# Moving three of the seven down-projection steps, and one hidden-layer copy, inside a feed-forward's step order

## The chip, the cores and the metric

The kernel runs on one core of a Trainium2 chip. The metric is the device time of one execution in microseconds (us), the median of several runs. Five engines work beside each other, each taking its own instructions strictly in the order in which they stand in the program for that engine: TensorE (PE, matrix products, with PEld for the loading of weights), VectorE (DVE), ScalarE (ACT), GpSimd (POOL) and SyncE (SP, which here issues DMA transfers). Products land in PSUM, which has eight banks of 128x512 fp32; everything else lives in SBUF.

## The reference

The reference is a two-layer decoder trunk on a sequence of 1024 tokens of width 1024, in fp32. Layer 0 mixes tokens with a sparse attention of three branches, layer 1 with dilated windows over shared keys and values. After each attention comes the same feed-forward, and that is where the change is:

```python
def swiglu(h, w_up, w_down):
    a, b = jnp.split(h @ w_up, 2, axis=-1)
    return (jax.nn.silu(a) * b) @ w_down
...
x = x + swiglu(rmsnorm(x, norm_ffn[layer]), ffn_w_up[layer], ffn_w_down[layer])
```

The hidden width is 2816, that is 22 inner blocks of 128 hidden columns.

## The kernel before, in words

Every fp32 operand of a product is split in two fp32r parts, a high one (`ph`, written by ACT, line 1002) and a low rest (`pl`, a subtraction on DVE, line 1003); `Pairs` at line 996 does that. One logical product of 128x128 by 128x512 is then three matmuls (`mm3`, lines 375 to 377: high x high, high x low, low x high).

The feed-forward (`ffn`, line 1369) takes the inner blocks two at a time. Both the up- and the down-projection are done as 2x2 block products in Strassen's form as Winograd wrote it, so seven products stand in place of eight.

**The hidden steps.** For each inner block j, `cols_steps` (line 1195) makes seven steps, in the order m1 m2 m5 m6 m7 m4 m3. Each is 12 matmuls: four products that add into one PSUM bank. m1, m6, m7 and m4 add into one bank, `ux` in the steady part; m2 has a bank `uy` for itself; m5 and m3 add into another tile of the same bank `uy`. The results are drained between: after m1, ACT copies the bank to `d0` (line 1218); after m2, DVE adds m2's bank to `d0` (line 1227) and ACT applies the SiLU (line 1415); after m6 and m7, ACT copies the bank again to `d1` and `c` (lines 1257, 1266), and DVE adds m5's bank to `c` (line 1267); after m4 and m3, DVE finishes (lines 1283 and 1417). The step m6 is fed by a GpSimd subtraction (line 1250), which overwrites the block that m5's operands are made from.

**The down steps.** The finished pair of blocks is four 128x512 tiles `u`, and four tiles `wd` hold its rows of the down-projection. `rows_steps` (line 1029) makes seven steps, called D0 to D6 here in the order in which `down_steps` (line 1431) leaves them. Each is 12 matmuls: four rows t, three matmuls each. D0, D3, D4 and D6 add into the four banks dx0 to dx3; D1, D2 and D5 use the two banks dr0 and dr1 in turn. After each row, DVE adds the bank to the residual stream `xr` (line 1061): four additions a step, and eight in D2. D2 and D3 are fed by four GpSimd operations each (lines 1069 to 1079). D0's preparation also issues the four weight transfers of its pair (`load_down`, line 1389), and, in layer 0, two transfers that another stage needs.

**The order.** The down steps of one pair are dealt out among the 14 hidden steps of the next pair. The loop at line 1460 builds one list `seq`, and `staged` (line 1019) runs it: the preparation of step k+1 (pairs, GpSimd operations, transfers) is written ahead of the products of step k. This is the written order. The build schedules it with a timeline simulation (`schedule_with_timeline_sim=True` in `kernel`): an instruction that the simulated timeline sees ready can go ahead of one written earlier, down to single matmuls, so that the order on an engine in the trace is near the written order and not equal to it. After the build each engine's order is fixed.

**The memory blocks.** `u` and the other temporaries are `scratch` blocks. `ut` deals out six of them (`scratch[7:13]`), four to a pair, so that the third and fourth tile of a pair, `u[2]` and `u[3]`, are the first and second tile of the pair before it, which the down steps are reading meanwhile. The second block of a pair has `base = 2` and keeps its `d0` in `u[2]`, its `d1` in `u[3]`. D3's preparation is the last reader of the old tile behind `u[2]`. `misc["c"]` is `scratch[13]`, the one block that holds `c` from m7 to m3.

In what follows the steps of the second block of a pair have a prime: m1', m2' and so on.

Of the kernel before, what the change touches and what calls it, by code (L numbers as in the profile page):

```python
# [299 lines left out]
def trunk(ctx, tc, I, out):  # L300
# [1068 lines left out]
    def ffn(p, scratch, B, xr, layer):  # L1369
# [4 lines left out]
        misc = dict(c=scratch[13], s1=scratch[14], s2=None)  # L1374
# [4 lines left out]
        def load_up(j, q, t=None):  # L1379

            t = wu() if t is None else t
            r, c = q % 2 * 512, q // 2 * FH + j * 128
            v = t.rearrange("p (a n) -> p a n", n=128)
            nc.sync.dma_start(v, up[r:r + 512, c:c + 128].rearrange("(a p) n -> p a n", p=128))
            k = q % 2 * 4
            nc.gpsimd.tensor_mul(v, v, gains[:, k:k + 4].unsqueeze(2).to_broadcast([128, 4, 128]))  # L1386
            raw.setdefault(j, []).append(t)
# [9 lines left out]
        def hidden(j, u):  # L1397

            def ahead(f):
                if j == 1:  # L1400
                    raw[2].clear()
                if 0 < j < NJ - 1:
                    for q in range(3):
                        load_up(j + 1, q)
                return f()

            def tmp(n):
                if n in ("d0", "d1"):
                    return u[base + int(n[1])]
                return scratch[15] if (j, n) == (0, "c") else misc[n]  # L1410

            def done(a, r, C):
                t = u[base + r]
                if a == 0:
                    nc.scalar.activation(t, C, AF.Silu)
                else:
                    nc.vector.tensor_mul(t, t, C)

            base = 2 * (j % 2)
            banks = {0: ("dx2", "uy", "uy"), 1: ("dx3", "ux", "uy")}.get(j, ("ux", "uy", "uy"))  # L1420
            steps = cols_steps(banks, "m1 m2 m5 m6 m7 m4 m3", pairs, tmp, B.ops, lambda: raw[j], done)
            i = 2 if j in (1, 2) else 0
            steps[i] = steps[i][0], lambda f=steps[i][1]: ahead(f)

            def m4(f=steps[5][1]):
                if j == 0:
                    raw[1].clear()
                if j + 1 < NJ:
                    for q in range(3 if j else 0, 4):
                        load_up(j + 1, q)  # L1430
                return f()
            steps[5] = "m4", m4
            return steps

        def down_steps(j, u):
            st = {}

            def first():
                w, last = load_down(j)
                if layer == 0 and 2 <= j < 18:  # L1440
                    for a in ((s1, LA, L1, W1 + 2), (s2, LA + L1, L2, W2 + 1)):
                        bias_skewed(*a, j - 2, last)
                st["s"] = rows_steps(("dr0", "dr1"), pairs, lambda s, i: own("t" + s), [(tuple(u), tuple(w))], xr)
                st["s"].insert(4, st["s"].pop(5))
                return st["s"][0]()

            return [first] + [lambda i=i: st["s"][i]() for i in range(1, 7)]
# [7 lines left out]
        seq, prev, pairs_of = [], [], {}  # L1455
# [4 lines left out]
        for j in range(0, NJ, 2):  # L1460
            if j >= 4:
                u = [ut() for _ in range(4)]
                pairs_of[j] = u, [hidden(j, u), hidden(j + 1, u)]
            u, us = pairs_of[j]
            if j == 0:
                norm = B.half(xr, 1, ("dr0", "dr1", "dx0", "dx1"),
                              ([own("ta")[:], own("tb")[:]] + wd.parts[:2],
                               wd.parts[2:3] + [scratch[10]] + scratch[12:14]),
                              sums=scratch[4:7] + scratch[15:])
                early = [us[1], pairs_of[2][1][0]]  # L1470
                us[0] = [("", f) for f in B.first_steps(us[0], norm, [f for c in early for _, f in c[:2]])]
                for c in early:
                    del c[:2]
            steps = [f for _, f in us[0] + us[1]]
            if j == 2:
                steps.insert(0, prev.pop(0))
            for i, f in enumerate(steps, j == 2):
                seq.append(f)
                if i % 2 and prev:
                    seq.append(prev.pop(0))  # L1480
            seq += prev
            prev = down_steps(j, u)
# [31 lines left out]
    def dense(layer, w, x_src, oT, tail, near, far):  # L1514

        lo, hi = slice(0, 512), slice(512, 1024)
        scratch = [oT[:, 4 * b + i, h] for h in (lo, hi) for b in range(2) for i in range(4)]
        with ExitStack() as c:
            c.push(open_banks(*[(n,) for n in ("dx0", "dx1", "dx2", "dr0", "dr1", "ux", "dx3", "uy")]))
            B = Blocks()  # L1520
            B.add(pool(c, "fb", far), ("B11", "B21"))
            xr = pool(c, "fx", far).tile([128, NT, D], F32, name="xr")
            out_proj(c, near, far, B, xr, oT, w, x_src, layer and 7)
            with ExitStack() as cu:
                p = pool(cu, "fu", near)
                with ExitStack() as ch:
                    B.add(pool(ch, "fb2", far), second)
                    last = ffn(p, scratch, B, xr, layer)
                with ExitStack() as ch:
                    pz = pool(ch, "fz", far)  # L1530
                    begin, finish = tail
                    last(pz, *begin(pz, B, xr))
            finish(c, B, xr, scratch)
# [436 lines left out]
```

## Time and profile before

| what | value |
|---|---|
| median of 3 runs | 2914.61 us (2912.68 to 2917.57) |
| profiled execution, its own time | 2911.7 us |
| its span, first to last instruction | 2909.9 us |
| granted TensorE clock, mean | 0.99 |
| PE busy, share of the span | 2817.3 us, 97% |
| DVE busy | 2255.6 us, 78% |
| ACT busy | 1520.9 us, 52% |
| POOL busy | 1540.8 us, 53% |
| feed-forward of layer 0, steady part | about 905 to 1428 us of the span |
| feed-forward of layer 1, steady part | about 2346 to 2868 us |

How to read it: matmuls are pipelined and their ends are modelled, so that a busy PE is not one at its peak. The number that tells is how fast matmuls follow each other: where nothing holds them up, 12 of them start within 2.72 us in these stages. In a timeline, a row is one instruction or a run of the same kind: start, duration, engine, line, operation, what it writes and reads, count, and in brackets the idle time before it and what ended it. In a table by windows, each row is a stretch of time with the busy time of each engine in it and the number of instructions.

### The profile page before, as it was taken

The page shows a single profiled execution, that of the slowest core. Times are in us where ns is not written, and L with a number is a line of the kernel's source. Part 1 is how long each engine was busy: PE and PEld are TensorE (multiplying, and loading weights), DVE is VectorE, ACT ScalarE, POOL GpSimd, SP SyncE. Part 2 cuts the span into 40 slices and gives each one's busy share as a digit, 9 for nine tenths or more (in the row PEclk, how much of TensorE's full clock was granted, in tenths as well). Part 3 has the DMA queues.
Part 4 walks back from the last instruction along what each step waited for, and adds up shares of the span by engine and source line. Part 5 has one row for each costly group of instructions (what it writes and reads, how often), then busy time and mean ns, then how long its engine had stood idle before and what let it go on. Part 6 is the DMA issues. An engine that isn't in the chain of part 4 may idle for free.

```text
span 2909.9 us, 43844 instructions
## 1 busy us (share of the span) xinstructions
PE 2817.3 (97%) x14766; PEld 2376.1 (82%) x14766; DVE 2255.6 (78%) x4465; ACT 1520.9 (52%) x3314; POOL 1540.8 (53%) x1776
## 2 busy tenths in 40 slices
PE   7999999999999999999999999899999999999997
PEld 6988899998877888888787888788877788888885
DVE  5441999997488888988876777598965888888887
ACT  5431888886443333333554444689855433333334
POOL 2134877873165555555546786455522655555551
PEclk8999999999999999999999999999999999999999
DMA  5756243212122322231225555966521221111112
GB/s 161 237 156 190 67 111 89 59 26 117 30 69 66 83 62 66 62 83 52 95 80 146 161 167 160 281 194 184 142 88 37 73 61 51 55 55 58 51 44 76
DMA packets 266833, 294.46 MB, mean 101 GB/s; under 512 B 18099, under 2 KB 209475, under 8 KB 266608
## 3 DMA queue, kind: packets, MB, share of 16 engines
q1 hardware_dynamic: 246960, 231.50, 27.5%
q0 software_dynamic: 19648, 60.16, 6.9%
q8 instruction: 117, 1.92, 0.3%
q14 instruction: 108, 0.88, 0.1%
HBM read 228.49 MB, written 78.81 MB: 106 GB/s over the span
## 4 chain that ended last, share of the span: by engine, by line
PE 72%; DVE 16%; ACT 4%; issue 3%; DMA 2%; POOL 2%; SPq 1%; DVEq 0%; ACTq 0%; POOLq 0%
PE ux L375 5%; PE ux L376 5%; PE ux L377 5%; DVE pl L1003 5%; PE pt L485 5%; DVE xr L1061 4%; PE uy L375 4%; PE uy L376 4%; PE uy L377 4%; PE dx L376 4%; PE dx L377 4%; PE dx L375 3%; PE dr L375 3%; PE mm L375 3%; PE mm L376 3%
## 5 line engine op out<-in xcount | busy, mean ns | idle before, releaser
L1003 DVE TENSOR_TENSOR pl<-oT,ph 128x512 fp32r<-128x512 f32 x325 | 323.6, 1016 | 73.2 <-ACT ph L1002 64.1
L1002 ACT ACTIVATE ph<-oT 128x512 fp32r<-128x512 f32 x325 | 196.4, 626 | 221.8 <-PE ux L376 60.2
L485 PE MATMUL pt<-ident,P 128*128 128x128 f32 x1536 | 260.3, 277 | 4.8 <-DVE tl L349 2.3
L1003 DVE TENSOR_TENSOR pl<-oTb,ph 128x512 fp32r<-128x512 f32 x235 | 218.2, 954 | 50.6 <-ACT ph L1002 42.3
L1002 ACT ACTIVATE ph<-oTb 128x512 fp32r<-128x512 f32 x235 | 140.4, 625 | 177.3 <-PE ux L376 52.5
L1061 DVE TENSOR_TENSOR xr<-xr,dr 128x512 f32<-128x512 f32 x320 | 204.6, 679 | 29.2 <-PE dr L377 29.2
L1386 POOL TENSOR_TENSOR oT<-oT,gffn 128x512 f32<-128x512 f32 x92 | 106.7, 1168 | 205.5 <-DMA oT<-in_ffn_w_up_dram 168.5
L349 DVE TENSOR_TENSOR tl<-pt,th 128x512 fp32r<-128x512 f32 (+1 forms) x320 | 194.2, 625 | 20.9 <-ACT th L348 17.3
L485 PEld LDWEIGHTS pt<-ident,P 128*128 128x128 f32 x1536 | 181.5, 141 | 28.3 <-POOL P L924 4.1
L924 POOL TENSOR_SCALAR P<-P,sm,gates 128x384 f32<-128x384 f32 (+7 forms) x256 | 182.6, 723 | 38.6 <-DVE sm L922 32.6
L1061 DVE TENSOR_TENSOR xr<-xr,dx 128x512 f32<-128x512 f32 x320 | 200.1, 680 | 2.4 <-PE dx L377 1.8
L348 ACT ACTIVATE th<-pt 128x512 fp32r<-128x512 f32 (+1 forms) x320 | 168.4, 545 | 42.9 <-PE pt L485 33.0
L1386 POOL TENSOR_TENSOR oTb<-oTb,gffn 128x512 f32<-128x512 f32 x92 | 103.8, 1138 | 154.5 <-DMA oTb<-in_ffn_w_up_dram 134.7
L920 ACT ACTIVATE P<-P,m 128x384 f32<-128x384 f32 (+7 forms) x256 | 171.1, 671 | 12.4 <-DVE m L918 9.0
L1761 ACT ACTIVATE P<-P,st 128x384 f32<-128x384 f32 (+2 forms) x256 | 139.4, 548 | 6.2 <-DVE st L1756 5.2
L376 PE MATMUL dx<-pl,ph 128*128 128x512 f32 x352 | 139.3, 396 | 1.0
L377 PE MATMUL dx<-ph,pl 128*128 128x512 f32 x352 | 136.5, 391 | 0.0
L510 PE MATMUL o<-tl,V 128*128 128x256 f32 x476 | 136.3, 304 | 0.0
L509 PE MATMUL o<-th,V 128*128 128x256 f32 x476 | 135.9, 300 | 0.2 <-DVE oTb L522 0.2
L1756 DVE CUSTOM_DVE_ANT_0 P<-s,T 128x384 f32<-128x384 f32 (+2 forms) x256 | 115.7, 478 | 15.9 <-PE s L1812 5.2
L1002 ACT ACTIVATE ph<-wd 128x512 fp32r<-128x512 f32 x86 | 53.7, 629 | 115.5 <-PE ux L376 55.0
L914 DVE CUSTOM_DVE_ANT_0 P<-s,T 128x256 f32<-128x256 f32 (+3 forms) x192 | 101.8, 551 | 6.4 <-PE s L912 4.6
(951 smaller groups left out, 9530.9 us busy)
## 6 DMA issues: line engine op xcount, KB each, us to landing
qB<-xr POOLq DMA_DIRECT2D x96, 256.0 KB, 5.1
oT<-in_ffn_w_up_dram SPq DMA_DIRECT2D x92, 256.0 KB, 3.1
oTb<-in_ffn_w_up_dram SPq DMA_DIRECT2D x92, 256.0 KB, 3.0
Q<-qB SPq DMA_DIRECT2D x40, 512.0 KB, 7.8
wd<-in_ffn_w_down_dram SPq DMA_DIRECT2D x66, 256.0 KB, 2.5
oT<-in_b_w_q_dram SPq DMA_DIRECT2D x48, 256.0 KB, 4.0
K<-kBs SPq DMA_DIRECT2D x40, 256.0 KB, 9.6
wraw<-in_a_w_in_dram SPq DMA_DIRECT2D x18, 512.0 KB, 4.7
```

What stands on the lines that cost most here:

```text
L348: nc.scalar.activation(H_, src, AF.Copy)
L349: nc.vector.tensor_sub(L_, src, f32(H_))
L375: nc.tensor.matmul(ps, lh, rh, start=first, stop=False, skip_group_check=bool(shared))
L376: nc.tensor.matmul(ps, lh, rl, start=False, stop=False, skip_group_check=bool(shared))
L377: return nc.tensor.matmul(ps, ll, rh, start=False, stop=last, skip_group_check=bool(shared))
L485: nc.tensor.transpose(ps[:, i * 128:(i + 1) * 128], b, ident)
L920: nc.scalar.activation(P[:, e, :n], P[:, e, :n], AF.Exp, bias=mm[:, e:e + 1], scale=-1.0, accum_out=sm[:, e:e + 1])
L924: nc.gpsimd.tensor_scalar(P[:, e, :n], P[:, e, :n], sm[:, e:e + 1], gt(g, t, br, 2 * hp + e, 1), op0=OP.mult, op1=OP.mult)
L1002: nc.scalar.activation(like(h), src, AF.Copy)
L1003: (eng or nc.vector).tensor_sub(like(l), src, f32(like(h)))
L1061: nc.vector.tensor_add(xs, xs, banks[t])
L1386: nc.gpsimd.tensor_mul(v, v, gains[:, k:k + 4].unsqueeze(2).to_broadcast([128, 4, 128]))
```

## The change

Two edits, both in `ffn`.

```diff
             def tmp(n):
+                if n == "d0" and j > 4 and j % 2:
+                    return misc["c"]
                 if n in ("d0", "d1"):
                     return u[base + int(n[1])]
                 return scratch[15] if (j, n) == (0, "c") else misc[n]
...
             for i, f in enumerate(steps, j == 2):
                 seq.append(f)
-                if i % 2 and prev:
+                if i in (2, 3, 5, 8, 10, 11, 13) and prev:
                     seq.append(prev.pop(0))
```

The written order for every pair from j = 4 on (nine pairs in each layer):

```
before: m1 m2 D0 m5 m6 D1 m7 m4 D2 m3 m1' D3 m2' m5' D4 m6' m7' D5 m4' m3' D6
after:  m1 m2 m5 D0 m6 D1 m7 m4 D2 m3 m1' m2' D3 m5' m6' D4 m7' D5 m4' m3' D6
```

D0, D3 and D4 each stand one hidden step later. For the pair j = 2, which has lost its first two hidden steps to an earlier place, the order starts with D0 in both versions, and there D1, D4 and D5 stand one step later. Nothing is added or taken away: the same matmuls, splits, additions and transfers are issued.

The other edit concerns the second block of each pair from j = 5 on. Its `d0`, the copy that ACT makes of m1', is kept in `misc["c"]` and no longer in `u[2]`; the SiLU then reads it there and writes `u[2]` as before. With D3 written behind m2', m1's copy into `u[2]` would be written ahead of D3's preparation, which still reads the old tile there.

## The prediction

> **What bounds the kernel now.** I read the page first, then the feed-forward in windows, then single engines in timelines. The page says that PE is the engine to watch:
>
> ```profile
> span 2909.9 us, 43844 instructions
> ...
> PE 2817.3 (97%) x14766; PEld 2376.1 (82%) x14766; DVE 2255.6 (78%) x4465; ACT 1520.9 (52%) x3314; POOL 1540.8 (53%) x1776
> ```
>
> A busy PE is no measure here, so I cut the steady feed-forward at the first matmul of m1 and of m1'. A first half (m1 to m1') holds 114 matmuls, which the weight loads count, and a second half 138. The windows of the first halves, one row and the sum of all 18 (16 with 114 loads, the pair j = 4 of each layer with 110):
>
> ```profile
> 1021.11:1046.98 25.87, 25.87 (x115) 21.42 (x114) 21.64 (x28) 9.24 (x16) 17.64 (x14) 1.00 0.17 52
> ...
> sum 463.72, PE 463.72 PEld 383.97 DVE 382.72 ACT 165.37 POOL 315.68; mean PE 25.76 PEld 21.33 DVE 21.26 ACT 9.19 POOL 17.54
> ```
>
> 25.87 us for 114 matmuls is 0.227 us each, 2.72 us for a step of 12: PE never waits there. The second halves that end in another pair's m1, one row and the sum of all 16:
>
> ```profile
> 1046.98:1079.84 32.86, 32.57 (x139) 25.68 (x138) 30.88 (x45) 12.81 (x22) 15.24 (x11) 1.00 0.32 80
> ...
> sum 518.20, PE 515.15 PEld 411.07 DVE 475.79 ACT 205.19 POOL 233.95; mean PE 32.20 PEld 25.69 DVE 29.74 ACT 12.82 POOL 14.62
> ```
>
> At 0.2267 us, 138 matmuls take 31.28 us, and 16 halves 500.5 us; they took 518.2. So PE loses 17.7 us there, 1.1 us a pair, and that is what a reordering can win. The timeline of PE shows one of the places, where D4 (`dx`) and m6' (`ux<-T2`) are cut into each other:
>
> ```profile
> 1056.54 1.01 PE L375 MATMUL dx<-ph 128*128 128x512 f32 x2
> 1057.66 0.50 PE L375 MATMUL ux<-T2h,ph 128*128 128x512 f32 x1
> 1057.99 0.39 PE L376 MATMUL ux<-T2l,ph 128*128 128x512 f32 x1
> 1058.22 0.62 PE L375 MATMUL dx<-ph 128*128 128x512 f32 x2
> 1058.92 0.50 PE L376 MATMUL dx<-pl,ph 128*128 128x512 f32 x1
> ```
>
> What they wait for is in DVE's timeline, which has no idle time in brackets: two `pl`, D3's four additions, and only then D4's `pl<-wd`, after which (1058.79) PE goes on; m2's addition, which frees `uy` for m5', is later still.
>
> ```profile
> 1054.50 1.29 DVE L1003 TENSOR_TENSOR pl<-oT,ph 128x512 fp32r<-128x512 f32 x2
> 1055.71 2.48 DVE L1061 TENSOR_TENSOR xr<-xr,dx 128x512 f32<-128x512 f32 x4
> 1058.10 0.77 DVE L1003 TENSOR_TENSOR pl<-wd,ph 128x512 fp32r<-128x512 f32 x1
> 1058.79 0.68 DVE L1003 TENSOR_TENSOR pl<-oT,ph 128x512 fp32r<-128x512 f32 x1
> 1059.39 0.67 DVE L1227 TENSOR_TENSOR oT<-oT,uy 128x512 f32<-128x512 f32 x1
> ```
>
> The windows from the end of m2' to the start of m5' (24 matmuls: D4 and m6'), one row and the sum of 16:
>
> ```profile
> 1056.50:1063.15 6.65, 6.43 (x26) 4.53 (x25) 6.65 (x12) 2.94 (x5) 4.83 (x5) 1.00 0.40 118
> ...
> sum 98.78, PE 96.93 PEld 69.98 DVE 98.78 ACT 45.60 POOL 70.50; mean PE 6.06 PEld 4.37 DVE 6.17 ACT 2.85 POOL 4.41
> ```
>
> 384 matmuls would take 87.0 us; they took 98.8, so 11.7 of the 17.7 us go here, 0.73 us a pair and 1.2 at most, and DVE is busy for all of the 98.78 us. The kernel is bound by PE, except where DVE is late, and that is at D4. Most of the rest is at m4', which waits for ACT's copy of the bank that m7' filled: a row of PE, and the windows from the last matmul of m7' to the second of m4' (5 matmuls), summed over the same 16 pairs.
>
> ```profile
> 1070.18 0.50 PE L375 MATMUL ux<-T4h,ph 128*128 128x512 f32 x1
> ```
>
> ```profile
> sum 23.67, PE 22.47 PEld 13.79 DVE 13.19 ACT 17.46 POOL 18.28; mean PE 1.40 PEld 0.86 DVE 0.82 ACT 1.09 POOL 1.14
> ```
>
> 80 matmuls would take 18.1 us, so 5.5 us are lost there.
>
> **The change part by part.** No instruction is added, so the sum is made of waits that go, stay or come.
>
> *D3 and D4 one step later.* What DVE has to do, counted from the code, as additions and `pl` of a step: D2 10; D0, D1, D3 to D6 6 each; m3 3; m2, m7, m4 2; m1, m5, m6 1: 70 over the 21 steps of a pair, 3.33 a step. How far the demand stands above its mean after each step, beginning at m1: before, it reaches +1.0 after D2, +1.0 after D3 and 0 after D4; after the change +1.0 after D2, -0.3 after D3 and -2.3 after D4, since m2' and m6', which ask little of DVE, now stand ahead of them. An operation costs DVE 0.60 us undisturbed (four additions from 1055.71 to 1058.10) and 0.75 in the mean: 21.64 + 30.88 us of the two rows above over 70. So DVE is ahead by 1.3 operations, 1.0 us, at D3 and 2.3 operations, 1.75 us, at D4. That is more than the mean and the worst stall at D4 (0.73 and 1.2 us). Also, m5' now has D3's 2.72 us between it and m2', in which its bank is freed; before, it had nothing. I take the whole stall: -11.7 us. Bounds: 0, if DVE's lateness moves with it, and -11.7.
>
> *m6' right behind m5' in the written order.* The GpSimd subtraction for m6' waits for m5's `pl`:
>
> ```profile
> 1055.27 1.67 POOL L1250 TENSOR_TENSOR oT<-oT 128x512 f32<-128x512 f32 x1 [7.16 <-DVE pl L1003]
> ```
>
> With 0.63 us on ACT and 0.68 on DVE this chain is 3.0 us, 0.3 more than one step. Started at 1055.27 as now, it is done at 1058.3. In the new order the same three steps m1', m2' and D3 are over at 1056.5, m5' takes until 1059.3, and m6' is due then, so I take 0. If m5's `pl` comes only just in time for m5', it costs 0.3 us a pair, 5.4 us for 18.
>
> *D0 behind m5.* D0 no longer stands between m2 and m5, which use the same bank `uy`. In DVE's timeline of a first half there is spare time just then:
>
> ```profile
> 1027.73 1.23 DVE L1003 TENSOR_TENSOR pl<-oT,ph 128x512 fp32r<-128x512 f32 x1 [2.06 <-ACT ph L1002]
> 1028.89 0.68 DVE L1227 TENSOR_TENSOR oT<-oT,uy 128x512 f32<-128x512 f32 x1
> ```
>
> The schedule can pull D0's matmuls ahead of m5, as it already let m6 pass m5. The one spot where the trace has m5 too near to m2 is the start of layer 0's feed-forward:
>
> ```profile
> 814.59 0.47 PE L375 MATMUL dx<-T2h,ph 128*128 128x512 f32 x1
> 815.92 0.50 PE L375 MATMUL uy<-T1h,ph 128*128 128x512 f32 x1 [0.85 <-DVE oT L1227]
> ```
>
> The step from one to the next is 1.33 us in place of 0.23: 1.1 us lost, and up to 1.2 with the slow second matmul behind a stall. Bounds 0 and +1.2 a pair; nearest is the first half as it is, with no loss, so I take 0.1, +1.8 us for 18 pairs.
>
> *m4'.* m7' D5 m4' is written as before: 0. Bound -5.5, if six of D5's matmuls come to stand between, 1.36 us, against four now.
>
> *The pair j = 2.* D5 waits 1.53 us for DVE (886.35 against 884.43: 1.7 us lost), and D2 0.83 us for its bank:
>
> ```profile
> 866.60 0.50 PE L375 MATMUL dr<-ph 128*128 128x512 f32 x1 [0.83 <-DVE xr L1061]
> ```
>
> ```profile
> 884.43 0.39 PE L376 MATMUL ux<-T2l,ph 128*128 128x512 f32 x1
> 886.35 0.50 PE L376 MATMUL dr<-pl,ph 128*128 128x512 f32 x1 [1.53 <-DVE pl L1003]
> ```
>
> D5 stands a step later, so half of 2 x 1.7 us goes (-1.7; bounds 0 and -3.4). D1 moves one step towards D2, with the same two banks: +0.8 (bounds 0 and +1.7).
>
> *`d0` in `misc["c"]`.* ACT's copy of m1' now waits until DVE has read `c`:
>
> ```profile
> 1050.90 0.69 DVE L1417 TENSOR_TENSOR oT<-oT 128x512 f32<-128x512 f32 x1
> ```
>
> ```profile
> 1051.30 0.58 ACT L1218 ACTIVATE oT<-ux 128x512 f32<-128x512 f32 x1
> ```
>
> The read ends at 1051.59, 0.3 us after the copy began. Queued behind it on ACT are two `ph`, whose `pl` DVE reached only at 1054.50; that hides it. 0; without that cover, 0.3 x 18 = +5.4 us.
>
> *Transfers and queues.* D0's four transfers, six in layer 0, pass m5, which issues none on SP. D0 has no GpSimd work; D3's four operations pass m2', which has none. D4 has none either. What D4 frees is the block of its second weight tile, refilled at once:
>
> ```profile
> 1058.89 0.34 SPq L1394 DMA_DIRECT2D wd<-in_ffn_w_down_dram  x1
> ```
>
> ```profile
> 1062.90 1.30 POOL L1070 TENSOR_TENSOR tb<-wd,wd 128x512 f32<-128x512 f32 x1
> ```
>
> A step later it is issued at 1061.6; the GpSimd operation that reads it would start 1 to 2 us later. Its result is wanted by the next pair's D2, some 30 us on: 0.
>
> *Sum:* -11.7 + 1.8 - 1.7 + 0.8 = -10.8 us. The profiled execution took 2911.7 us, 1.8 more than its span, so it becomes 2900.9. The median of the runs is 2.9 us above that execution, so the median becomes 2903.8, and I say 2904. A change under 0.2%, 5.8 us, can't be told from none.
>
> **The rivals.**
>
> *All of it goes.* D4 now stands ahead of m7', so that D5's matmuls may all fall between m7' and m4', and the order m7', six of `dr`, m4' runs without loss in the first halves. For it: those halves lose nothing. Against it: D5 is written where it was. -11.7 - 5.5 - 3.4 = -20.6: 2894.
>
> *The lateness moves along.* DVE is busy for 475.79 of 518.20 us in the second halves, 92%. If its backlog there is made by the long `pl` and not by the order, the same 0.7 us is lost at m5' or m6':
>
> ```profile
> L1003 DVE TENSOR_TENSOR pl<-oT,ph 128x512 fp32r<-128x512 f32 x20 | 20.9, 1070 | 2.1 <-ACT ph L1002 2.1
> L1061 DVE TENSOR_TENSOR xr<-xr,dx 128x512 f32<-128x512 f32 x17 | 10.6, 679 | 0.0
> ```
>
> In one pair the `pl` take 1070 ns in the mean, the additions 679. Against it: the lead of 1.75 us at D4. 2914 to 2916.
>
> *It does nothing.* The schedule sets the machine's order from what is ready, and may give nearly the old one: 2914.6. Against it: between steps that are all ready, the written order decides.
>
> *Slower: m5 waits for m2's bank.* If the schedule keeps m5 in front of D0, or DVE's addition comes later on the chip than the schedule thought, PE stands at m5 in the first halves, 1.2 us by the row at 815.92, 21.6 us for 18 pairs in place of my 1.8. From 12.6 / 18 = 0.7 us a pair it eats the gain. 2903.8 - 1.8 + 21.6 = 2923.6. Against it: the spare 2.06 us on DVE. The Trainium skill (Perfetto Trace Analysis, section Optimizing Tensor Performance) speaks for this rival: independent groups of matmuls should rotate through PSUM banks, so that one group is drained while the next one computes, and here two groups on one bank come to stand side by side. The stall at 815.92 agrees with it.
>
> **How the numbers follow.** My forecast 0.43, all goes 0.14, moves along 0.22, nothing 0.05, slower 0.16. So faster 0.57, same 0.27, slower 0.16. The forecast's own range is 2898 to 2909, from the gain at m4' coming as well to just under half of the stall at D4 staying. The range for 8 in 10 takes in the unchanged cases and the better one, and of the slower one the part up to 0.3 us a pair over break-even: 2893 to 2920.
>
> **What would show it.** Right: D3 stands between m2' and m5' on PE, D4 is not cut into m6', the second halves fall from 32.4 to about 31.7 us, and the first halves stay within 0.1 us of 25.9. Wrong: `uy<-T1` in a first half with idle time ended by DVE's line 1227; second halves still at 32.4 us, with DVE busy throughout at another place; ACT waiting for line 1417 ahead of line 1218 and PE behind it.

## The result, and the profile after

The changed kernel takes 2898.09 us (median of 4 runs, 2897.33 to 2901.70) against 2915.27 us (4 runs, 2912.68 to 2917.57): 17.2 us less, a ratio of 0.9946 with a 95% interval of 0.9934 to 0.9958. The forecast was 2904, range 2893 to 2920, and faster at 0.57. So the direction and the mechanism held, and the gain was larger than the 10.8 us of the sum.

The profiled execution of the changed kernel took 2901.7 us against 2911.7 before, only 10.0 us less. Windows show why the two comparisons differ. The rows are the feed-forward of layer 0, all between the two feed-forwards, and the feed-forward of layer 1, from the first matmul of m1 in the bank `ux` to the last matmul of the last m4'. The kernel before:

```profile
808.71:1421.34 612.63, 606.76 (x2661) 491.99 (x2662) 536.45 (x732) 237.73 (x410) 345.28 (x255) 1.00 0.25 68
1421.34:2248.86 827.52, 793.76 (x4436) 675.51 (x4434) 612.95 (x1326) 510.60 (x1222) 449.78 (x597) 0.99 0.50 149
2248.86:2861.60 612.74, 606.88 (x2661) 491.95 (x2662) 531.84 (x732) 237.62 (x410) 331.04 (x248) 1.00 0.18 56
```

The changed kernel:

```profile
807.79:1413.18 605.39, 601.55 (x2662) 492.74 (x2662) 554.65 (x732) 237.47 (x410) 352.72 (x255) 1.00 0.26 69
1413.18:2246.33 833.15, 795.66 (x4437) 676.17 (x4435) 619.00 (x1326) 509.81 (x1222) 450.12 (x598) 0.98 0.49 148
2246.33:2851.58 605.25, 601.34 (x2662) 493.06 (x2663) 550.89 (x732) 237.49 (x410) 337.66 (x248) 1.00 0.19 56
```

The two feed-forwards fell from 1225.4 to 1210.6 us, by 14.7. The part between them took 5.6 us longer in this one execution. In it PE waited 4.31 us once, for a `pl` that took DVE 3.89 us, where a `pl` with GpSimd idle takes 0.68 in the feed-forwards. For 3 us behind that wait the matmuls start 0.43 us apart, at a granted clock of 0.50 (see the last section). Why this one `pl` took so long is not shown. GpSimd waited 5.8 us for a weight transfer of another stage near there, but that wait ended at 1677.95, ten microseconds after PE's, and so is not its cause.

```profile
1667.39 0.50 PE L377 MATMUL dr<-B21h,pl 128*128 128x512 f32 x1 [4.31 <-DVE pl L1003]
```

```profile
1663.44 3.89 DVE L1003 TENSOR_TENSOR pl<-oT,ph 128x512 fp32r<-128x512 f32 x1
```

The stretch does not belong to the change: over the profiles of this study it lay between 827.5 and 836.4 us, and in another profile of the changed kernel it was 827.55 us, as before. So below, feed-forwards are compared with feed-forwards.

The second halves of the changed kernel, one row and the sum of the 16 that the prediction summed, then the sum of the 18 first halves:

```profile
1043.23:1074.88 31.65, 31.58 (x140) 25.83 (x138) 30.69 (x43) 12.80 (x22) 12.73 (x10) 1.00 0.37 83
...
sum 506.44, PE 505.25 PEld 413.23 DVE 490.56 ACT 204.95 POOL 241.60; mean PE 31.58 PEld 25.83 DVE 30.66 ACT 12.81 POOL 15.10
```

```profile
sum 465.93, PE 465.93 PEld 384.88 DVE 406.61 ACT 167.10 POOL 323.55; mean PE 25.89 PEld 21.38 DVE 22.59 ACT 9.28 POOL 17.97
```

518.20 has become 506.44, 11.8 us less. The first halves lose as little as before: they hold 8 more matmuls (1.8 us; in the pairs j = 4 a third of a `dx` step moved in), and so only 0.4 us of their 2.2 are new. In PE's timeline, D3 stands between m2' and m5'. D4 is still cut into m6', three matmuls of it, which the prediction had expected to end, but nobody waits:

```profile
1055.47 0.39 PE L375 MATMUL ux<-T2h,ph 128*128 128x512 f32 x1
1055.70 0.39 PE L376 MATMUL ux<-T2l,ph 128*128 128x512 f32 x1
1055.92 0.84 PE L375 MATMUL dx<-ph 128*128 128x512 f32 x3
1056.60 0.39 PE L377 MATMUL ux<-T2h,pl 128*128 128x512 f32 x1
...
1058.87 0.39 PE L375 MATMUL dx<-ph 128*128 128x512 f32 x1
1059.10 0.39 PE L376 MATMUL dx<-pl,ph 128*128 128x512 f32 x1
```

DVE's timeline beside it:

```profile
1050.51 0.68 DVE L1227 TENSOR_TENSOR oT<-oT,uy 128x512 f32<-128x512 f32 x1
1051.59 1.88 DVE L1061 TENSOR_TENSOR xr<-xr,dx 128x512 f32<-128x512 f32 x3 [0.41 <-PE dx L377]
1053.39 0.68 DVE L1003 TENSOR_TENSOR pl<-oT,ph 128x512 fp32r<-128x512 f32 x1
1053.99 0.68 DVE L1061 TENSOR_TENSOR xr<-xr,dx 128x512 f32<-128x512 f32 x1
1054.59 0.68 DVE L1003 TENSOR_TENSOR pl<-oT,ph 128x512 fp32r<-128x512 f32 x1
1055.19 1.53 DVE L1003 TENSOR_TENSOR pl<-wd,ph 128x512 fp32r<-128x512 f32 x1
```

m2's addition is done at 1051.2, before m5' needs the bank at 1052.75. At D3 DVE even waits for PE, 0.41 us, and D4's `pl<-wd` ends at 1056.7, 2.4 us before the matmul that needs it. Before, PE stood there.

### The profile page after: what moved, and what is told of

Its sections match the earlier page's. It is cut to its first block, busy times and chain, and to the rows that moved or that the text cites. A ratio compares the mean times of both kernels' runs of the same rounds, so it can differ in the third digit from the quotient of the medians.

```text
span 2899.9 us, 43941 instructions
## 1 busy us (share of the span) xinstructions
PE 2807.6 (97%) x14766; PEld 2378.1 (82%) x14766; DVE 2298.3 (79%) x4465; ACT 1519.7 (52%) x3314; POOL 1555.0 (54%) x1776
## 4 chain that ended last, share of the span: by engine, by line
PE 80%; DVE 8%; ACT 3%; POOL 3%; DMA 2%; issue 2%; SPq 1%; DVEq 0%; POOLq 0%; ACTq 0%
PE ux L375 6%; PE ux L376 6%; PE ux L377 6%; PE uy L375 5%; PE uy L376 5%; PE uy L377 5%; PE pt L485 5%; PE dx L375 4%; PE dx L376 4%; PE dx L377 4%; PE dr L375 3%; PE dr L377 3%; PE dr L376 3%; PE mm L375 3%; PE mm L376 3%; PE mm L377 3%
## 5 line engine op out<-in xcount | busy, mean ns | idle before, releaser
L1003 DVE TENSOR_TENSOR pl<-oT,ph 128x512 fp32r<-128x512 f32 x325 | 344.0, 1074 | 64.7 <-ACT ph L1002 49.8
L1003 DVE TENSOR_TENSOR pl<-oTb,ph 128x512 fp32r<-128x512 f32 x235 | 229.7, 996 | 43.8 <-ACT ph L1002 27.6
L375 PE MATMUL mm<-hH,wh 128*128 128x512 f32 (+1 forms) x264 | 103.5, 393 | 0.7 <-DVE hL L352 0.6
```

Source lines behind the costliest of these rows:

```text
L375: nc.tensor.matmul(ps, lh, rh, start=first, stop=False, skip_group_check=bool(shared))
L1003: (eng or nc.vector).tensor_sub(like(l), src, f32(like(h)))
```

## The experiments

Twelve more runs were made. "Feed-forwards" is the sum of the two windows as above, from each kernel's own profile: 1225.4 us before, 1210.6 and, in another execution, 1211.2 with the change. Kernels with an added argument have their line numbers one higher. The runs come from three comparisons, in which the kernel before had medians of 2915.2, 2913.3 and 2913.2 us, so the ratios tell more than the medians.

| kernel | ratio to the kernel before, 95% interval | median, us | feed-forwards, us |
|---|---|---|---|
| changed kernel, again | 0.9942 [0.9928, 0.9956] | 2897.2 | 1211.2 |
| only `d0` in `misc["c"]` | 0.9994 [0.9982, 1.0006] | 2914.0 | 1226.5 |
| D3 and D4 moved, D0 not | 0.9943 [0.9923, 0.9962] | 2899.3 | 1210.4 |
| D0 alone | 0.9983 [0.9973, 0.9993] | 2908.8 | 1222.1 |
| D4 alone | 1.0008 [0.9997, 1.0019] | 2918.3 | 1228.8 |
| D3 alone | 0.9984 [0.9970, 0.9999] | 2910.2 | 1221.8 |
| old order, less work on DVE | 0.9953 [0.9939, 0.9968] | 2895.0 | 1206.7 |
| m5 forced ahead of D0 | 1.0212 [1.0182, 1.0243] | 2969.7 | 1279.2 |
| D5 one step later too | 1.0020 [1.0006, 1.0033] | 2918.0 | 1229.8 |
| another order for j = 2 | 0.9966 [0.9953, 0.9979] | 2903.0 | 1212.1 |
| D3's `pl` on GpSimd | 0.9964 [0.9949, 0.9978] | 2904.1 | 1215.0 |
| that, and D5 held behind m7' | 0.9985 [0.9972, 0.9997] | 2909.7 | 1219.1 |

**The change once more.**

> The changed kernel once more, beside the kernel before and the next three. The first comparison gave a gain of 17 us by the medians, while the feed-forwards of the two profiles account for 14.7. My theory: the rest is the scatter of other stages, and the feed-forwards take 1210 to 1211 us again (from the first m1 of the steady part to the last m4', both layers) against 1225; time ratio 0.993 to 0.996.

The feed-forwards took 1211.2 us and the ratio was 0.9942. Both came as expected: the gain of the feed-forwards is 14 to 15 us, and the rest of the 17 lies within the interval of the ratio, which reaches from 12 to 19 us in the first comparison.

**Only the copy.**

```diff
-                if i in (2, 3, 5, 8, 10, 11, 13) and prev:
+                if i % 2 and prev:
```

> The old order of steps, with only the second block's d0 kept in misc["c"]. My theory: ACT's copy of m1' starts up to 0.3 us later, behind DVE's read of c, and DVE's backlog hides it; PE's order is the old one and its losses stay at 0.7 us a pair at D4 and 0.35 us at m4', so within 3 us of the kernel before. Rival (the copy in the shared block holds ACT up, and PE behind it): 0.3 us more in each of the 18 pairs, about 5 us slower than before.

No difference that can be measured. PE's order near D4 is the old one, and so are its losses. No run moves D3 without this copy, so whether the copy is needed is not shown. In the changed kernel's profile the wait for DVE's read of `c` is there, and its length is the 0.3 us of the prediction:

```profile
1047.09 0.60 ACT L1218 ACTIVATE oT<-ux 128x512 f32<-128x512 f32 x1 [0.30 <-DVE oT L1419]
```

**D3 and D4 without D0.**

```diff
-                if i in (2, 3, 5, 8, 10, 11, 13) and prev:
+                if i in (1, 3, 5, 8, 10, 11, 13) and prev:
```

> The changed kernel with D0 put back to its old place behind m2 (and, in the pair j = 2, D1). My theory: the gain comes from D3 and D4 alone, D0 is worth nothing, since the first halves lost nothing before or after: within 2 us of the changed kernel's 2898. Rival (D0's move gives DVE an earlier start into the second half): the loss at D4 comes back in part, at least 0.3 us a pair, 2904 or more.

It is as fast as the whole change, and its feed-forwards take 1210.4 us. D0's move is not needed beside the others.

**D0 alone**, on the kernel before:

```diff
-                if i % 2 and prev:
+                if i in (2, 3, 5, 7, 9, 11, 13) and prev:
```

> The kernel before with only D0 one step later (and D1 of the pair j = 2). My theory: worth nothing, the second halves lose 1.1 us a pair as before: within 3 us of the kernel before. Rival (later work on D0 frees DVE for the second half): at least 0.3 us a pair gained, 2909 or less.

2908.8 us is just what the rival named, and the feed-forwards gained 3.2 us. So my "nothing" was too little: the second halves lost 0.6 to 1.5 us in place of 0.7 to 1.6. The effect is small, and with D3 and D4 moved nothing is left of it.

**D4 alone**, on the kernel before:

```diff
-                if i % 2 and prev:
+                if i in (1, 3, 5, 7, 10, 11, 13) and prev:
```

> The kernel before with only D4 one step later (and D5 of the pair j = 2). Theory of DVE's lead: when D4 starts, DVE has 2.3 operations less to do than before, 1.75 us, as in the changed kernel; the stall of 0.7 us a pair at D4 goes, so 2899 to 2903. Theory of the bank: the stall comes from m5' standing right behind m2' on the same bank, which makes PE take D4 as a filler before its operands are there; D3 doesn't stand between them here, so 0.5 us or more a pair is lost again after m2', 2909 or more.

The theory of the lead fails here as I had put it. The order on PE became m2', m6', four matmuls of D4, m5', the rest of D4. D4 itself lost nothing. But m6', now right behind m2', waited, and the second halves lost 0.8 to 2.0 us each, by PE's timeline:

```profile
1057.81 0.40 PE L375 MATMUL ux<-T2h,ph 128*128 128x512 f32 x1
1058.04 0.40 PE L376 MATMUL ux<-T2l,ph 128*128 128x512 f32 x1
1058.94 0.50 PE L377 MATMUL ux<-T2h,pl 128*128 128x512 f32 x1 [0.50 <-DVE pl L1003]
```

and DVE's timeline has D3's four additions ahead of the `pl` it wanted:

```profile
1055.51 2.47 DVE L1061 TENSOR_TENSOR xr<-xr,dx 128x512 f32<-128x512 f32 x4
1057.90 0.99 DVE L1003 TENSOR_TENSOR pl<-oT,ph 128x512 fp32r<-128x512 f32 x1
```

The bank was the rival's reason, and its time came true, but the wait is for DVE's backlog and not for the bank. With D3 at its old place, whatever follows m2' meets that backlog.

**D3 alone.**

```diff
-                if i in (2, 3, 5, 8, 10, 11, 13) and prev:
+                if i in (1, 3, 5, 8, 9, 11, 13) and prev:
```

> The changed kernel with only D3 one step later; D0 and D4 stand where they stood before (the pair j = 2 has only its D4 later). Theory of DVE's lead: DVE's demand by D4 is what it was before, so the stall of 0.7 us a pair stays near D4: 2911 to 2915. Theory of the bank: D3 between m2' and m5' gives the bank 2.72 us to be drained, D4 is no filler any more, and the stall goes: 2898 to 2902.

Neither theory by its number: 2910.2 us. D4 lost nothing any more, as the theory of the bank had it. The lateness came back one down step on, at D5, in 13 of the 16 second halves (0.5 to 1.7 us each; three lost nothing), by PE's timeline:

```profile
1065.79 0.50 PE L376 MATMUL dr<-pl,ph 128*128 128x512 f32 x1 [0.49 <-DVE pl L1003]
```

and in DVE's, D4's four additions and three long `pl`:

```profile
1062.58 2.47 DVE L1061 TENSOR_TENSOR xr<-xr,dx 128x512 f32<-128x512 f32 x4
1064.97 2.81 DVE L1003 TENSOR_TENSOR pl<-oT,ph 128x512 fp32r<-128x512 f32 x3
```

So each move alone passes the stall on, and of these orders only the one with both takes it away.

**Less work on DVE, old order.** D2's additions to the upper half of the stream are left out, so the down-projection is incomplete there.

```diff
-                step(T, 0, [(1, 1), (0, 1)], sums1),
+                step(T, 0, [(1, 1)], sums1),
```

> The kernel before, with the old order of steps, but D2 adds its banks to the residual stream at one place and not at two: four of DVE's 70 operations of a pair are left out, and that half of the down-projection is incomplete. PE has the same matmuls. Theory that DVE's lateness is the cause: DVE has 2.4 to 3 us less to do ahead of D4, so the stall at D4 and m6' (0.7 us a pair) goes with the old order too, and the second halves fall to at most 31.7 us: 2899 to 2904. Theory of the bank alone (D4 as a filler between m2' and m5'): the stall at D4 stays at 0.5 us a pair or more, 2910 or more.

It runs as fast as the changed kernel, with the old written order. In PE's timeline m2' is followed by two matmuls of D4, two of m6' and ten of D4, the same cut as before, and now without a pause:

```profile
1051.43 0.61 PE L375 MATMUL dx<-ph 128*128 128x512 f32 x2
1051.89 0.39 PE L375 MATMUL ux<-T2h,ph 128*128 128x512 f32 x1
1052.12 0.39 PE L376 MATMUL ux<-T2l,ph 128*128 128x512 f32 x1
1052.34 0.62 PE L375 MATMUL dx<-ph 128*128 128x512 f32 x2
1052.80 0.39 PE L376 MATMUL dx<-pl,ph 128*128 128x512 f32 x1
```

The window of this second half:

```profile
1041.91:1073.21 31.30, 31.30 (x140) 25.90 (x138) 26.72 (x38) 13.14 (x22) 15.02 (x12) 1.00 0.37 84
```

DVE has 26.7 us to do in place of 30.9, and PE loses nothing in 31.30 us; the other 15 second halves lose nothing either. This is the clearest of the runs: taking four operations from DVE removes the stall that the change removes. One caution: the build's schedule sees the smaller load too, and D5 and D6 were cut differently: six matmuls of D5 stand between m7' and m4' there, so that the loss at m4' is gone too. At D4 the order was the same.

**m5 forced ahead of D0.** PE may take D0's and m6's matmuls only behind m5's.

```diff
-                        mm3(banks[t], part(a, t), b, i == 0 and onX != 2, i == n - 1, onX)
+                        with after(wait() if onX == 1 else None):
+                            mm3(banks[t], part(a, t), b, i == 0 and onX != 2, i == n - 1, onX)
...
-                blk(held("x", nx), a, "T2", False)
+                blk(held("x", nx), a, "T2", False, ops["m5"])
```

`wait` gives m5's last matmul.

> The changed kernel with two orders laid down on PE: D0's matmuls, and those of m6, may not go ahead of m5's, so that m5 follows m2 directly in every first half, on the same bank. My rival of the slower side, forced: PE waits for DVE's addition of m2's bank, 1.1 to 1.2 us in each of the 18 first halves, 20 to 21 us: 2917 to 2920. Against it (DVE drains the bank while the next weights load): under 0.3 us a pair, 2903 or less.

The rival was real, and dearer than its price: 54 to 56 us slower than before, about 70 over the changed kernel, 3 to 4 us a pair. In PE's timeline of a first half:

```profile
1035.07 0.80 PE L375 MATMUL uy<-T1h,ph 128*128 128x512 f32 x1 [2.68 <-DVE oT L1228]
1035.67 0.63 PE L376 MATMUL uy<-T1l,ph 128*128 128x512 f32 x1
```

and in DVE's:

```profile
1032.90 1.52 DVE L1003 TENSOR_TENSOR pl<-oT,ph 128x512 fp32r<-128x512 f32 x1
1034.34 0.68 DVE L1228 TENSOR_TENSOR oT<-oT,uy 128x512 f32<-128x512 f32 x1
```

The addition to be waited for stands behind long `pl` on DVE; the row at the start of the feed-forward, from which I priced it, had none. And after a wait of that length the matmuls themselves are slow (see the last section). The Trainium skill (Perfetto Trace Analysis, section Optimizing Tensor Performance) has independent groups rotate through banks; this run agrees with it. In the changed kernel the schedule did it: PE's order in the first halves is m2, D0, m6, m5, although m5 is written ahead of D0. It was the same in the kernel before, but for one matmul of m6.

**D5 later.**

```diff
-                if i in (2, 3, 5, 8, 10, 11, 13) and prev:
+                if i in (2, 3, 5, 8, 10, 12, 13) and prev:
```

> The changed kernel with D5 one step later, behind m4', to take the loss at m4' (0.35 us a pair) away. My theory: six of D5's matmuls now go between m7' and m4' in one piece, 1.36 us, which covers ACT's copy; second halves at 31.3 us, 6 us faster than the changed kernel, 2892. Rival (DVE's lateness moves along: D5 and D6 now stand close, and the next first half begins with DVE behind): first halves lose 0.3 us or more each, 2897 or more.

The feed-forwards are 19 us longer than with the change, and the gain is gone. Six matmuls of D5 did come to stand between m7' and m4', but the third waited for DVE: the second halves lost 0.8 to 2.0 us each. The next first halves lost 0.1 to 1.0 us in layer 0 as well.

```profile
1067.66 0.50 PE L376 MATMUL dr<-pl,ph 128*128 128x512 f32 x1 [0.90 <-DVE pl L1003]
```

**Another order for j = 2.**

```diff
-                if i in (2, 3, 5, 8, 10, 11, 13) and prev:
+                if i in ((3, 5, 6, 8, 10, 11) if j == 2 else (2, 3, 5, 8, 10, 11, 13)) and prev:
```

> The changed kernel with another order for the pair j = 2 alone: D1 behind m6, D2 behind m4, D3 behind m3, the rest as in the changed kernel. The one stall left there, 1.6 us at m7 in each layer, waits for a pl on DVE. My theory: with D1 a step later DVE reaches m7's pl in time; 2 to 3 us faster than the changed kernel, 2895 to 2896. Rival: the stall moves to D2's bank or to D3, as large as before; 2898.

The rival came true: the stall at m7 went, and others came behind D3 of that pair, at D4, D5, m3' and the next m1. They sum to 3.0 us in layer 0 and 1.9 in layer 1, against 1.7 at m7 in each layer of the changed kernel. The feed-forwards take 1212.1 against 1210.6 us.

**D3's `pl` on GpSimd.**

```diff
-                step(T, 2, [(0, 1)], sums2),
+                step(T, 2, [(0, 1)], sums2, eng=(nc.gpsimd, nc.gpsimd)),
```

> The changed kernel with D3's two low parts (pl) made on GpSimd and not on DVE, which leaves DVE 68 operations a pair. Theory that the 0.35 us at m4' are ACT's copy and too few matmuls behind m7', and not DVE's lateness: they stay, second halves at 31.65 us, within 2 us of the changed kernel. Theory that DVE is behind this loss too: second halves near 31.3 us, up to 6 us faster than the changed kernel. A price of GpSimd's longer operations would show as new idle time of PE at D3.

The window of a second half:

```profile
1046.74:1078.43 31.69, 31.61 (x139) 25.82 (x138) 29.14 (x41) 12.81 (x22) 17.07 (x14) 1.00 0.36 83
```

DVE has 1.5 us less to do and the half is no shorter. So the 0.35 us at m4' are not DVE's lateness. They are the copy on ACT behind too few matmuls: in the run with less work on DVE, where six matmuls stand there in place of four, they are gone. The theory's number was missed: the feed-forwards are 4.4 us longer than the changed kernel's, since the pair j = 2 got slower by 1.7 to 1.9 us in each layer. Nothing was won.

**The same, with D5 held behind m7'.**

```diff
+                        with after(wait() if late else None):
...
-                step((A(2), B(3)), 0, [(0, 1)]),
+                step((A(2), B(3)), 0, [(0, 1)], late=True),
```

> The same, and D5's matmuls may not go ahead of m7', so that six of them stand between m7' and m4'. The run with D5 written later gave PE that order too, and lost 1.2 us a pair waiting for D5's pl. Theory of DVE's lateness: with two operations less DVE is 1.2 to 1.5 us earlier, D5's pl are there, the copy is covered, second halves at 31.3 us: 6 us faster than the changed kernel. Rival: GpSimd's extra work lengthens the pl beside it by as much, and D5 waits again, 0.5 us a pair or more: slower than the changed kernel.

Half of the theory came true, and the time is the rival's: 2909.7 us, and feed-forwards 8.5 us longer than the changed kernel's. Two windows, the rest of a first half and the second half that follows, in layer 0:

```profile
1020.81:1046.93 26.12, 25.26 (x111) 20.57 (x110) 23.93 (x30) 8.37 (x15) 18.60 (x14) 1.00 0.18 51
1046.93:1078.49 31.56, 31.56 (x139) 25.82 (x138) 29.65 (x41) 12.70 (x22) 16.34 (x13) 1.00 0.36 84
```

Twelve of the 16 second halves fell to 31.3 us (the row above is one of the other four), in layer 1 with first halves that lose only 0.1 us. In layer 0, 110 matmuls of a first half take 26.1 us in place of 24.9: the lateness moved into D0. Why it is layer 0 alone stays open. No version that computes the whole result beat the changed kernel; the one without D0's move equals it.

## Why the prediction was right, and where its sizes were off

The terms of the sum, in us, beside what the feed-forwards of the first profile show:

| term | forecast | measured |
|---|---|---|
| D4 and m6', 16 second halves | -11.7 | -11.8 |
| D4 of the last pair in each layer, left out of the sum | 0 | -0.5 |
| m6' right behind m5' | 0 | 0 |
| D0 behind m5 | +1.8 | +0.4 |
| m4' | 0 | 0 |
| j = 2, D5 | -1.7 | -3.6 |
| j = 2, D1 closer to D2 | +0.8 | +0.7 |
| `d0` in `misc["c"]` | 0 | 0 |
| sum | -10.8 | -14.7 |

The measured terms are rounded one by one. The +0.4 is all that the first halves lost beyond their eight added matmuls.

*The bound and the main term* were right. The whole 11.7 us came, and DVE's lateness was the cause, as the run with less work on DVE shows. One sign was wrong: D4 is still cut into m6'.

The working behind the term, a count of operations over the written order, was right for the whole change and wrong as a rule: by it D4 alone should have done, and D4 alone was no faster than the kernel before. It had D4 behind m5', at its mean, and said that m5' had nothing between it and m2'. The prediction's own rows show D4 and m6' right behind m2'. In that order the same count stands 2.3 operations above its mean after D4 before the change and 2.3 below it after, a lead of 4.7 operations and not 2.3. So there was luck in it: the count over the wrong order erred to the safe side. Even in PE's order it does not mark every stall. With D4 alone m6' waits where the count is 2.7 below its mean, and with D5 later D5 waits at 1.0 below. What held PE there was the `pl` that it needed, behind other operations in DVE's queue. The run with D3 alone shows the other half: the backlog is passed on to a later step, unless the moves give room at both.

*Mis-sized: D5 of the pair j = 2.* I halved the stall of 1.7 us for want of a row. It went altogether: the half from m1' on has 120 matmuls in 27.20 us.

*Mis-sized: D0 behind m5.* 0.1 us a pair was a guess above zero; the schedule pulled D0 ahead and it cost nothing. The bound of +1.2 for the case that it does not was far too low, since the forced run paid 3 to 4.

*D1 closer to D2* came out at its number for another reason. The wait for the bank at D2 is gone, and in its place m7 waits once:

```profile
861.76 0.50 PE L377 MATMUL ux<-T3h,pl 128*128 128x512 f32 x1 [1.32 <-DVE pl L1003]
```

*m4'* kept its loss: 0.46 us from the last matmul ahead of it to its first in the kernel before, 0.47 after, where 0.23 is undisturbed:

```profile
1065.23 0.50 PE L375 MATMUL ux<-T4h,ph 128*128 128x512 f32 x1
```

The rival in which all of it goes failed here. The rival in which the lateness moves along was wrong for the change, and right for D4 alone, for D3 alone, for D5 later and for j = 2.

*From the sum to the median* I added the 2.9 us by which the earlier profile lay under its median. The later profile lay 3.6 us above its own, and its stretch between the feed-forwards was 5.6 us longer. The 2.5 us between the 14.7 of the terms and the 17.2 of the medians belong to no term; the interval of the ratio, 12 to 19 us, holds both. So 3.9 of the 5.7 us by which the forecast of 2903.8 was too high are the terms, and the other 1.8 are of the size of the scatter of the runs.

## What to carry to other kernels

Where one engine is nearly full and another fills for some microseconds at a time, find the operation that PE stands waiting for and what lies ahead of it in the full engine's queue. Moving steps that ask much of that engine behind steps that ask little can win without a single operation less. A sum of its operations step by step against their mean is a guide to such moves and no proof: do it in the order that the machine has after the build, since here it misled for single moves. Look one step past the place that is mended, since a backlog that is only passed on costs about as much there. A profile's own time can lie some microseconds off its median for a stage that has nothing to do with the change, so compare the stage before the whole.

## What the runs showed of the hardware that was not expected

A wait of 2 us on PE can cost more than itself. In the run with m5 forced ahead, the windows around the wait show the granted clock in the third column from the end:

```profile
1031.00:1034.00 3.00, 1.39 (x7) 0.81 (x5) 3.00 (x3) 0.63 (x1) 2.87 (x2) 1.00 0.01 1
1035.00:1036.00 1.00, 0.93 (x2) 0.83 (x3) 1.00 (x2) 0.63 (x1) 0.92 (x2) 0.50 0.02 6
1036.00:1037.00 1.00, 1.00 (x4) 0.71 (x4) 0.38 (x1) 0.00 (x0) 1.00 (x1) 0.50 0.00 0
1037.00:1038.00 1.00, 1.00 (x4) 0.81 (x3) 0.00 (x0) 0.00 (x0) 0.52 (x1) 0.51 0.00 0
1038.00:1039.00 1.00, 1.00 (x6) 0.83 (x5) 0.00 (x0) 0.00 (x0) 0.00 (x0) 1.00 0.00 0
```

After 2.68 us of idle time the clock is 0.50 for another 2.7 us or so, and the matmuls start 0.43 us apart in place of 0.23, which adds some 1.5 us. That run has 25 waits of PE in the feed-forwards that were longer than 0.7 us. The ten of 1.48 us or less were never followed by a lower clock; of the fifteen of 2.05 to 2.84 us, twelve were, sometimes a few matmuls late. The longest was not, so that the length alone does not decide. The Trainium skill (TensorE: Matmul & The Clock Gate, section What's actually happening) puts the drop after an idle window of about 3.4 us that runs on its own; here 2.05 us sufficed. The stalls that the change removed were at most 1.53 us of idle time at once and had no such tail, so their price was little more than their length: 1.8 us lost for those 1.53.

DVE got busier without more work: in the 18 first halves 406.6 us against 382.7, in the 16 second halves 490.6 against 475.8. Its operations on SBUF alone were longer where GpSimd worked beside them: in the changed kernel a `pl` takes 0.68 us with GpSimd idle, and 1.25 to 1.4 us in the mean, at most 1.79, beside a GpSimd operation, while its additions from PSUM take 0.68 us either way. PE did not pay for it, since DVE was ahead.
